# A row softmax with tiles in three buffers: later first store and 16 KB packets for the last stores

## The chip, the cores and the metric

The kernel runs on one core of a Trainium2 chip. The metric is the device time of one execution in microseconds (us), and the median of several is quoted. A profile is one traced execution, so its span differs from the median by a few microseconds.

## The reference

```
batch, seq, vocab = 16, 256, 32768          # 4096 rows of float32
scaled = logits / temperature               # temperature = 1.0
scaled = scaled - scaled.max(axis=-1, keepdims=True)
exp_scaled = np.exp(scaled)
return exp_scaled / exp_scaled.sum(axis=-1, keepdims=True)
```

536.87 MB are read and as much is written.

## The kernel before

Each row of 32768 is cut into two halves on two neighbouring partitions, so that 64 tiles of 128 partitions x 16384 values (8.39 MB) pass through three buffers. A tile is loaded through SyncE's queue, goes through DVE (VectorE, the maximum) and ACT (ScalarE, the exponential) piece by piece, has its sums joined, is scaled on both engines and is stored through ScalarE's queue. A load into a buffer waits for the store that empties it. Tiles 0 and 63 are loaded in four pieces, and tile 63 is also stored in four; all others move in one transfer of 64 KB per partition.

```
def load(t):
    n = _END if t in (0, G - 1) else _LOAD        # 4096 or 16384 columns
    for s in range(0, W, n):
        nc.sync.dma_start(out=buf[t % _BUFS][:, s : s + n], in_=x[...])

def store(t, a, b):
    nc.scalar.dma_start(out=o[t * P : (t + 1) * P, a:b], in_=buf[t % _BUFS][:, a:b])

def normalise(t):
    for k in range(K):
        nc.vector.tensor_reduce(out=nm[:, k : k + 1], in_=xc, axis=X, op=A.max, negate=True)
        nc.scalar.activation(out=xc, in_=xc, func=Exp, bias=nm[:, k : k + 1], ...)
    # ... the sums of the two halves are joined, f is the factor of each piece ...
    for k in range(K):
        # DVE scales columns a:b, ACT scales b:c
        if t == G - 1:
            store(t, a, c)
    if t < G - 1:
        store(t, 0, W)

for t in range(_BUFS):
    load(t)
for t in range(G):
    normalise(t)
    if t + _BUFS < G:
        load(t + _BUFS)
```

## Time and profile before

| | before |
|---|---|
| median of 3 runs | 2516.56 us |
| span of the profile | 2510.7 us |
| DVE, ACT busy | 63%, 54% |
| queues of loads and stores, share of 16 DMA engines | 49.7%, 49.6% |

Two rows of the page suffice to see what kind of kernel this is: the compute engines are idle for a third to a half of the time and the DMA engines are never idle but at the end. What can be gained has to be sought in the stretches of time in which the DMA engines move less than their steady rate.

### The profile page before, as it was taken

The numbers are of one execution on the slowest core, as the hardware profiler recorded it, in microseconds if no ns is written. First come the engines' busy times: TensorE is split into PE (matmuls) and PEld (weight loads), VectorE is DVE, ScalarE is ACT, GpSimd is POOL, SyncE is SP. The second block draws the span as 40 slices with busy tenths as digits, with TensorE's granted clock in tenths as the row PEclk, the third lists the DMA queues.
The fourth block names the chain that finished last, engine by engine and source line by source line (L and its number), as shares of the span: only waits on it lengthen the run. The fifth ranks groups of instructions, "written<-read, shape, count | busy, mean of one in ns | idle before, by whom it ended". The sixth has DMA issues, their size and how long they took to land.

```text
span 2510.7 us, 2617 instructions
## 1 busy us (share of the span) xinstructions
DVE 1575.7 (63%) x1216; ACT 1368.1 (54%) x895; POOL 0.2 (0%) x4
## 2 busy tenths in 40 slices
DVE  6465766657656666576665665766656657666573
ACT  6445646546455465564554645645546456465463
POOL 0000000000000000000000000000000000000000
DMA  9999999999999999999999999999999999999996
GB/s 401 389 427 434 433 433 434 434 433 434 435 433 434 434 432 423 434 434 432 434 434 433 434 433 433 434 434 434 433 434 434 434 433 434 432 427 434 434 427 296
DMA packets 19748, 1073.91 MB, mean 428 GB/s; under 512 B 2192, under 2 KB 2192, under 8 KB 2192
## 3 DMA queue, kind: packets, MB, share of 16 engines
q1 hardware_dynamic: 10080, 536.88, 49.7%
q10 hardware_dynamic: 9648, 536.88, 49.6%
q14 instruction: 20, 0.16, 0.0%
HBM read 536.87 MB, written 536.87 MB: 428 GB/s over the span
## 4 chain that ended last, share of the span: by engine, by line
DMA 72%; DVE 17%; ACT 9%; another core or an unknown queue 2%; issue 0%; SPq 0%; ACTq 0%
DMA x<-in_logits_dram 36%; DMA out_dram<-x 35%; DVE nm L99 12%; ACT x L106 7%; DVE x L135 4%; ACT x L139 2%; DVE f L131 0%; ACT ee L116 0%; DVE rS L130 0%; DVE Sh L78 0%; DVE ttj L119 0%; DVE Sh L75 0%; SPq L62 0%; ACTq L68 0%
## 5 line engine op out<-in xcount | busy, mean ns | idle before, releaser
L99 DVE TENSOR_REDUCE nm<-x 128x1 f32<-128x4096 f32 x318 | 1117.6, 3579 | 701.6 <-DMA x<-in_logits_dram 701.6
L106 ACT ACTIVATE x<-x,nm 128x4096 f32<-128x4096 f32 x318 | 965.4, 3036 | 1043.5 <-DVE nm L99 1043.5
L139 ACT ACTIVATE x<-x,f 128x2048 f32<-128x2048 f32 (+1 forms) x194 | 371.2, 1975 | 75.1 <-DVE f L131 73.7
L135 DVE TENSOR_SCALAR x<-x,f 128x4096 f32<-128x4096 f32 (+2 forms) x194 | 372.2, 1975 | 2.5 <-DVE f L131 0.2
L119 DVE CUSTOM_DVE_ANT_0 ttj<-ee,ssum 128x5 f32<-128x5 f32 (+1 forms) x64 | 10.6, 166 | 196.7 <-ACT ee L116 196.7
L106 ACT ACTIVATION_READ_ACCUMULATOR x<-x,nm 128x1 f32 x318 | 59.3, 186 | 0.0
L116 ACT ACTIVATE ee<-nm,nMh 128x5 f32<-128x5 f32 (+1 forms) x64 | 18.2, 284 | 0.0
L131 DVE TENSOR_SCALAR f<-ee,rS 128x5 f32<-128x5 f32 (+1 forms) x64 | 14.8, 231 | 2.2
L130 DVE RECIPROCAL rS<-Sh 128x1 f32<-128x1 f32 x64 | 10.5, 164 | 2.2
L78 DVE TENSOR_TENSOR nMh<-nMh 128x1 f32<-128x1 f32 x64 | 10.2, 159 | 2.2
L78 DVE TENSOR_TENSOR Sh<-Sh 128x1 f32<-128x1 f32 x64 | 10.2, 159 | 2.2
L114 DVE TENSOR_REDUCE nMh<-nm 128x1 f32<-128x5 f32 (+1 forms) x64 | 10.1, 157 | 2.2
L75 DVE STREAM_SHUFFLE Sh<-Sh 128x1 f32<-128x1 f32 x64 | 9.7, 151 | 0.0
L75 DVE STREAM_SHUFFLE nMh<-nMh 128x1 f32<-128x1 f32 x64 | 9.7, 151 | 0.0
L106 ACT ACT_TABLE_LOAD x1 | 1.3, 1283 | 8.1 <-DMA x<-in_logits_dram 8.1
L119 DVE DVE_READ_ACCUMULATOR2_ANT Sh<- 128x1 f32 x64 | 5.2, 82 | 0.0
L75 DVE LOAD_MASK_SELECT nMh<-nMh x64 | 0.9, 14 | 2.8
L75 DVE LOAD_MASK_SELECT Sh<-Sh x64 | 0.9, 14 | 2.8
L170 POOL MEMSET const-bfloat16-1.0<- 128x1 bf16 x1 | 0.1, 102 | 0.0
L170 POOL MEMSET const-uint8-127<- 128x1 uint8 x1 | 0.1, 102 | 0.0
L170 POOL MEMSET const-float32-0.0<- 128x1 f32 x1 | 0.1, 99 | 0.2 <-issue 0.2
L170 POOL MEMSET const-float32-1.0<- 128x1 f32 x1 | 0.1, 99 | 0.0
## 6 DMA issues: line engine op xcount, KB each, us to landing
x<-in_logits_dram SPq DMA_DIRECT2D x8, 2048.0 KB, 23.7
out_dram<-x ACTq DMA_DIRECT2D x4, 2048.0 KB, 10.7
out_dram<-x ACTq DMA_DIRECT2D x63, 44.3
x<-in_logits_dram SPq DMA_DIRECT2D x62, 43.6
```

The costliest lines, as they stand in the source:

```text
L75: nc.vector.stream_shuffle(out=v[:, j + 1 : j + 2], in_=v[:, j : j + 1], mask=mask)
L78: nc.vector.tensor_tensor(out=v[:, j + 1 : j + 2], in0=v[:, j : j + 1], in1=v[:, j + 1 : j + 2], op=op,)
L99: nc.vector.tensor_reduce(out=nm[:, k : k + 1], in_=xc, axis=X, op=A.max, negate=True)
L106: nc.scalar.activation(out=xc, in_=xc, func=Exp, bias=nm[:, k : k + 1], scale=inv_t, accum_out=ssum[:, k : k + 1],)
L114: nc.vector.tensor_reduce(out=nMh[:, 0:1], in_=nm, axis=X, op=A.min)
L116: nc.scalar.activation(out=ee, in_=nm, func=Exp, bias=nMh[:, n_rounds : n_rounds + 1], scale=-1.0)
L119: nc.vector.tensor_tensor_reduce(out=ttj, in0=ee, in1=ssum, scale=1.0, scalar=0.0, op0=A.mult, op1=A.add, accum_out=Sh[:, 0:1],)
L130: nc.vector.reciprocal(out=rS, in_=Sh[:, n_rounds : n_rounds + 1])
L131: nc.vector.tensor_scalar_mul(out=f, in0=ee, scalar1=rS)
L135: nc.vector.tensor_scalar_mul(out=xs[:, a:b], in0=xs[:, a:b], scalar1=f[:, k : k + 1])
L139: nc.scalar.activation(out=xs[:, b:c], in_=xs[:, b:c], func=Copy, scale=f[:, k : k + 1])
L170: nc = _bacc.Bacc("TRN2", target_bir_lowering=False, num_devices=1)
```

## The change

The intent is to keep the first store out of the way of the first loads, and to let the last load and the last stores share the DMA engines evenly. Store 0 is put behind the first exponential of tile 1 in ScalarE's program. The stores of tiles 61 and 62 go in four transfers of 16 KB per partition. The loads are called one step later, which changes nothing in SyncE's order.

```
+_FINE_STORES = 3
     def store(t: int, a: int, b: int) -> None:
-        nc.scalar.dma_start(
-            out=o[t * P : (t + 1) * P, a:b], in_=buf[t % _BUFS][:, a:b]
-        )
+        n = _END if t >= G - _FINE_STORES else b - a
+        for s in range(a, b, n):
+            nc.scalar.dma_start(
+                out=o[t * P : (t + 1) * P, s : s + n],
+                in_=buf[t % _BUFS][:, s : s + n],
+            )
 ...   (in the loop of exponentials)
+            if t == 1 and k == 0:
+
+                store(0, 0, W)
 ...
-        if t < G - 1:
+        if 0 < t < G - 1:
             store(t, 0, W)
 ...
-            if t + _BUFS < G:
-                load(t + _BUFS)
+            if t and t + _BUFS - 1 < G:
+                load(t + _BUFS - 1)
```

## The prediction

> **What bounds the kernel now.** I read the page first, because it says in two lines that this is a transfer problem: DVE is busy 63% and ACT 54% of the span, while the DMA row is at 9 in all but the last of 40 slices, and the two queues together fill 99.3% of what 16 DMA engines could do.
>
> ```profile
> DVE 1575.7 (63%) x1216; ACT 1368.1 (54%) x895; POOL 0.2 (0%) x4
> ...
> GB/s 401 389 427 434 433 433 434 434 433 434 435 433 434 434 432 423 434 434 432 434 434 433 434 433 433 434 434 434 433 434 434 434 433 434 432 427 434 434 427 296
> ...
> q1 hardware_dynamic: 10080, 536.88, 49.7%
> q10 hardware_dynamic: 9648, 536.88, 49.6%
> ```
>
> The GB/s row shows where anything is to be had. The plateau is 434; the second slice (389) and the last (296) stand out, and the first holds the launch. All bytes, 1073.76 MB, at 434 GB/s take 2474 us, against a span of 2510.7: only 36.6 us are not plateau, and no compute saving can matter. So I cut the span into stretches (columns: window, length, busy time of each engine with instruction counts, clock, DMA share, GB/s).
>
> ```profile
> 40.00:104.00 64.00, 37.33 (x22) 28.95 (x18) 0.00 (x0) 1.00 0.95 365
> 104.00:160.00 56.00, 31.88 (x34) 30.43 (x22) 0.00 (x0) 1.00 1.01 437
> 160.00:2418.00 2258.00, 1432.26 (x1105) 1243.01 (x815) 0.00 (x0) 1.00 1.00 433
> 2418.00:2448.00 30.00, 24.67 (x20) 21.35 (x14) 0.00 (x0) 1.00 0.97 416
> 2448.00:2474.00 26.00, 12.92 (x3) 11.40 (x6) 0.00 (x0) 1.00 0.90 386
> 2474.00:2490.00 16.00, 8.62 (x14) 6.40 (x5) 0.00 (x0) 1.00 0.05 22
> ```
>
> Two holes. Between 40 and 104 us the rate is 365 although DMA is 95% busy: (434-365)/434 x 64 = 10.2 us lost to slow packets, not to idleness. Between 2474 and 2490 DMA is idle: (434-22)/434 x 16 = 15.2 us. The timeline of the end names the second hole:
>
> ```profile
> 2447.85 13.06 DVE L99 TENSOR_REDUCE nm<-x 128x1 f32<-128x4096 f32 x3
> 2448.01 0.34 ACTq L68 DMA_DIRECT2D out_dram<-x  x1
> ...
> 2477.43 4.42 DVE L99 TENSOR_REDUCE nm<-x 128x1 f32<-128x4096 f32 x1 [16.51 <-DMA x<-in_logits_dram]
> ...
> 2488.78 0.34 ACTq L68 DMA_DIRECT2D out_dram<-x  x1
> ```
>
> Three of the last tile's four pieces are reduced by 2460.9, then DVE waits 16.5 us for the fourth, and the first store of the last tile is issued 11.35 us after that piece (2488.78 - 2477.43). By then the store of tile 62 (issued 2448.01) is through, so nothing fills the DMA engines. Why is piece four late? The DMA view of 2420 to 2432, while the last load and the store of tile 61 share the engines (columns: packets, MB, share):
>
> ```profile
> q10 hardware_dynamic: 64, 4.19, 80.8%
> q1 hardware_dynamic: 64, 1.05, 20.4%
> ```
>
> Equal numbers of packets, but a store packet is 64 KB and a load packet of the last tile 16 KB: the load gets a fifth of the bytes. The same recurs after 2450 against the store of tile 62. In the DMA records 13 of 16 engines finish piece four within 5.5 us of the first, the last three 14.9, 17.8 and 25.7 us after it. They had lagged by 5 to 7 us in the preceding tiles and met the 64 KB stores again.
>
> **What the Trainium skill says.** "DMA: Bandwidth & Descriptors", section "Queues, rings and completion order": each DMA engine goes round-robin between the queue rows it has work for and switches only at packet boundaries. The trace agrees: 64 packets against 64 above. Section "Where 436 GB/s comes from" gives 435.2 GB/s as the ceiling of the port fabric; the plateau of 433 to 437 is it, so the middle cannot improve. Section "Rules for kernel authors" says that spreading DMAs over issuing engines buys no bandwidth; here the queues stay SyncE and ScalarE before and after, so I give that nothing. No page I found explains 365 GB/s at 95% busy.
>
> **The change part by part.** The order listing shows SyncE's sequence of loads unchanged: moving the call for the next load after the tile that follows keeps the same buffers and the same wait on the same store. DVE does not change. On ACT, one store moves and two become four pieces each. Bytes are equal.
>
> Part one, fine stores of tiles 61 and 62 (63 already had four): six more issues at 0.34 us, 2.0 us on an ACT queue that waits anyway; 16 KB packets move 425 to 431 GB/s in the trace where they run alone, against 434, which over some 25 MB is well under 1 us. The gain: the last load is issued around 2415.2 to 2418.0 and its data start near 2418. Now packets are equal, so it gets half of 434. On the three late engines the previous load ends at 2420; from there their shares of the last load and of store 61 are 2 x 0.524 MB at 27.1 GB/s an engine (434/16), 38.7 us, so piece four lands near 2458 instead of 2477. Adding 11.35 us, the first store of tile 63 is issued near 2470, with 1.5 us to its first packet 2471.5. The thirteen prompt engines then have their share of store 62 done near 2450.5 + 19.3 = 2470, a gap of 1.5 us; the late three get it done near 2458 + 19.4 = 2477.5 and have no gap. The last 8.39 MB take 19.4 us (0.524 MB an engine): 2497, and the landing 2497.5. Against 2510.7 that is **-13 us**. It is below the 15.2 us of the hole because the late engines end it.
>
> Part two, the held store. Store 0 is issued at 38.28 and its packets appear as load 2 begins; from there to 104 both directions are slow: in the trace's records the packets take 2.9 us (load) and 2.7 us (store) in place of 2.418. After the change it comes behind the first exponential of tile 1, which starts at 46.49 and lasts 3.71, so it is issued near 50.3, 12 us later. Load 2 (42 to 61 alone at 434) keeps the engines full meanwhile, so holding costs no idle time: 10 us x 434 = 4.3 of its 8.39 MB pass alone. The mixed stretch shrinks from some 44 us to some 20, and the two streams no longer start together. If the slowness belongs to that lock-step start, 10.2 us come back, and the lag of three engines with it (up to 6 us at the end, since the slowest engine ends the kernel). If slowness belongs to the first so many microseconds of mixed traffic, load 3 with store 1 will pay it later and nothing is won. I choose 6 of a possible 16 us. Sum: 13 + 6 = 19, from 2516.6 to **2497 us**, -0.8%.
>
> **Rivals.** First: only the tail gains; the slow stretch moves from 42-104 to about 52-120. For it speaks a second slow patch in the records at about 94 to 102, when load 3 meets store 1 at another phase; against it, that in 2258 us of mixed traffic afterwards the rate is 433. It makes 2503. Second: both come back in full, the engines stay in step, and the tail is one solid stream: 2516.6 - 13 - 16 = 2488. Third: equal shares help the load but delay store 61 and store 62, and the hole shifts instead of closing. The DMA work is conserved, and store 62 still has 2458 to 2477 to fill on the late engines, so I expect at most 2 us of gap; were half the hole left, some 7 us less gain, 2504. Fourth: the held store delays load 3 and thereby starves tile 3. Load 3 waits for store 0, which would land near 81 instead of 91.5, when its load is issued now, as there is less to share with; the buffer cycle (store 44.2, load 43.5, compute 28, sum 116 = three tiles of 38.6) has slack only in DMA queueing, and DMA is never empty, so I see no loss; if wrong, up to +10, 2507.
>
> **Range and chances.** The tail is arithmetic on measured packets, good to some 4 us; the start is nearly a coin toss between 0 and 16. That gives 2486 to 2506. A gain of 2% would need 50 us where only 36.6 are off the plateau, launch and first landing included, so faster by 2% is all but excluded; slower by 2% needs a new stall of 50 us that I cannot see.
>
> **What would show it.** Right: the windows after show no 22 GB/s stretch between the last load and the last store; DVE's wait for the last piece falls from 16.5 us to 10 or less; in the stretch where load 63 meets store 61, packets and bytes of both queues are equal; the stores of 61 and 62 are eight issues more of 2048 KB; the rate at 40 to 104 rises above 400. Wrong: the hole stays with equal shares (piece four was late for another reason); the second slice of the GB/s row stays below 400 or the third falls (slow mixed traffic only moved); or a plateau slice falls below 430.

## The result

| | before | after |
|---|---|---|
| median of 4 runs each | 2516.01 us | 2497.87 us |
| lowest to highest | 2514.04 to 2518.52 | 2495.30 to 2502.61 |
| span of the profile | 2510.7 us | 2493.4 us |

The ratio is 0.993, with a 95% interval of 0.9912 to 0.9947. The kernel is 18 us faster and within 2% of before, as predicted.

First the page of the changed kernel, the row of GB/s in 40 slices and the two queues:

```profile
GB/s 421 433 424 436 435 437 424 436 434 437 424 436 435 437 424 436 433 428 435 434 430 433 434 436 427 433 436 431 429 435 437 423 435 437 427 431 437 425 429 379
...
q10 hardware_dynamic: 10512, 536.88, 49.9%
q1 hardware_dynamic: 10080, 536.88, 49.9%
```

The second slice rose from 389 to 433 and the last from 296 to 379. But the middle, which was at 432 to 435 in all but a few slices, now has slices of 423 to 429 again and again. The stretches of time of the changed kernel (same columns as in the prediction; the windows at the end are moved to where its last tile is):

```profile
40.00:104.00 64.00, 49.24 (x38) 42.70 (x28) 0.00 (x0) 1.00 1.00 426
104.00:160.00 56.00, 24.62 (x19) 21.35 (x14) 0.00 (x0) 1.00 1.00 430
160.00:2410.00 2250.00, 1427.73 (x1102) 1238.33 (x812) 0.00 (x0) 1.00 1.00 433
2413.00:2443.00 30.00, 26.63 (x20) 21.35 (x14) 0.00 (x0) 1.00 1.00 429
2443.00:2464.00 21.00, 15.75 (x8) 10.44 (x5) 0.00 (x0) 1.00 1.01 432
2464.00:2474.00 10.00, 4.99 (x10) 7.88 (x8) 0.00 (x0) 1.00 0.41 174
```

The slow stretch at 40 to 104 is gone: 426 in place of 365, worth (426-365)/434 x 64 = 9.0 us. The hole at the end is smaller, not closed: 10 us at 174 cost (434-174)/434 x 10 = 6.0 us, where the prediction said 1.5 on most engines and nothing on the late ones. The DMA view of the changed kernel, 2420 to 2432, answers to the 64 against 64 packets of before (packets, MB, share; a record of 4 bytes per engine and transfer is counted too):

```profile
q1 hardware_dynamic: 184, 2.75, 53.5%
q10 hardware_dynamic: 176, 2.42, 47.3%
```

Packets are about equal and so, now, are bytes: 2.75 MB of the last load against 2.42 MB of the store. Before it was 1.05 against 4.19. The last engine's share of piece four is in 1.1 us after the first engine's, in place of 25.7. So the even sharing worked, and yet a hole is left. ScalarE's timeline at the end of the changed kernel (start, duration, instruction, idle time before it) says why:

```profile
2437.55 0.34 ACTq L71 DMA_DIRECT2D out_dram<-x  x1
2439.03 1.99 ACT L146 ACTIVATE x<-x,f 128x2048 f32<-128x2048 f32 x1
2439.82 13.70 ACTq L71 DMA_DIRECT2D out_dram<-x  x3
2453.56 3.71 ACT L110 ACTIVATE x<-x,nm 128x4096 f32<-128x4096 f32 x1 [12.54 <-DMA x<-in_logits_dram]
...
2471.52 0.34 ACTq L71 DMA_DIRECT2D out_dram<-x  x1
```

Each issue takes 0.34 us, but the last three of tile 62 span 13.70 us, and behind them ScalarE begins the last tile's first exponential only at 2453.56, when the last piece of the load has landed. What it waits for stands in the listing of the compiled program. A transfer raises a completion semaphore, a counter, when it has landed. The program hands out eight of them in turn, named DMAHW0 to 7; the last load's pieces raise 7, 0, 1 and 2, and the four stores of tile 62, which come eight transfers later, get the same and wait for them:

```
445 L71 DMACopy out_dram<-x_60 128x4096 [waits DMAHW7_49,DVE_49]
446 L71 DMACopy out_dram<-x_60 128x4096 [waits DMAHW0_49,DVE_49]
447 L71 DMACopy out_dram<-x_60 128x4096 [waits DMAHW1_49,DVE_49,Activation_49]
448 L71 DMACopy out_dram<-x_60 128x4096 [waits DMAHW2_49,Activation_49]
```

The trace agrees to a tenth of a microsecond. The second line is the last piece of the load in the view of the chain that ended last (issue and time to landing); it lands at 2411.84 + 41.26 = 2453.10, and the fourth store is issued 0.08 us later. The third is issued at 2443.46, and piece three had landed at 2443.36.

```profile
2443.46 0.34 ACTq L71 DMA_DIRECT2D out_dram<-x  x1
...
2411.84 41.26 DMA x<-in_logits_dram
...
2453.18 0.34 ACTq L71 DMA_DIRECT2D out_dram<-x  x1
```

In the kernel before, 67 stores in place of 73 were spread so that no store met such a wait late. The same wait held tile 61's third store too, from 2403.4 until tile 62's load had landed (2412.99; issue at 2413.08). There it delayed no exponential: the first maximum of tile 62 was ready only at 2417.4. The four exponentials of the last tile, which could have followed the load piece by piece, now run one after another from 2453.56 to 2468.34, and the first store of that tile is issued at 2471.52: 18.4 us after the last piece landed (2453.1), against 11.35 before.

### The profile page after: what moved, and what is told of

Same layout as the page of the kernel before. It is cut to its first block, busy times and chain, and to the rows that moved or that the text cites. A ratio compares the mean times of both kernels' runs of the same rounds, so it can differ in the third digit from the quotient of the medians.

```text
span 2493.4 us, 2622 instructions
## 1 busy us (share of the span) xinstructions
DVE 1575.8 (63%) x1216; ACT 1367.7 (55%) x895; POOL 0.2 (0%) x4
## 4 chain that ended last, share of the span: by engine, by line
DMA 75%; DVE 15%; ACT 9%; issue 0%; SPq 0%; DVEq 0%; ACTq 0%
DMA x<-in_logits_dram 38%; DMA out_dram<-x 37%; DVE nm L103 11%; ACT x L110 7%; DVE x L142 3%; ACT x L146 2%; DVE f L138 0%; SPq L63 0%; ACT ee L123 0%; DVE rS L137 0%; DVE Sh L82 0%; DVE ttj L126 0%; DVE Sh L79 0%; DVEq L191 0%; ACTq L71 0%
## 5 line engine op out<-in xcount | busy, mean ns | idle before, releaser
L126 DVE CUSTOM_DVE_ANT_0 ttj<-ee,ssum 128x5 f32<-128x5 f32 (+1 forms) x64 | 10.6, 166 | 203.0 <-ACT ee L123 203.0
L123 ACT ACTIVATE ee<-nm,nMh 128x5 f32<-128x5 f32 (+1 forms) x64 | 18.1, 283 | 0.0
L137 DVE RECIPROCAL rS<-Sh 128x1 f32<-128x1 f32 x64 | 10.5, 164 | 2.2
L82 DVE TENSOR_TENSOR nMh<-nMh 128x1 f32<-128x1 f32 x64 | 10.2, 160 | 2.2
L82 DVE TENSOR_TENSOR Sh<-Sh 128x1 f32<-128x1 f32 x64 | 10.2, 159 | 2.2
## 6 DMA issues: line engine op xcount, KB each, us to landing
x<-in_logits_dram SPq DMA_DIRECT2D x8, 2048.0 KB, 18.4
out_dram<-x ACTq DMA_DIRECT2D x61, 44.3
```

Of the source, the lines that this page charges most:

```text
L82: nc.vector.tensor_tensor(out=v[:, j + 1 : j + 2], in0=v[:, j : j + 1], in1=v[:, j + 1 : j + 2], op=op,)
L123: nc.scalar.activation(out=ee, in_=nm, func=Exp, bias=nMh[:, n_rounds : n_rounds + 1], scale=-1.0)
L126: nc.vector.tensor_tensor_reduce(out=ttj, in0=ee, in1=ssum, scale=1.0, scalar=0.0, op0=A.mult, op1=A.add, accum_out=Sh[:, 0:1],)
L137: nc.vector.reciprocal(out=rS, in_=Sh[:, n_rounds : n_rounds + 1])
```

## The experiments

Two yardsticks made the runs comparable although the time up to tile 62 varies by some 15 us between the profiles. The **tail** is the span less the start of DVE's first reduction of tile 62, which is the moment its load has landed; the **front** is that start itself. The slow packets of the middle are counted from the trace's DMA records: what 64 KB packets between 160 and 2400 us took above the usual 2.418 us each, summed and divided by 16 engines.

| profile | store 0 | stores 61, 62 | front | tail | slow packets in the middle |
|---|---|---|---|---|---|
| before | at once | 64, 64 KB | 2420.0 | 90.7 | 5.1 |
| e6 | at once | 64, 64 KB | 2422.0 | 90.7 | 6.0 |
| e10 | at once | 64, 64 KB | 2422.4 | 90.5 | 8.2 |
| e2 | at once | 16, 16 KB | 2426.3 | 80.5 | 13.5 |
| e11 | at once | 16, 16 KB | 2421.2 | 80.6 | 9.0 |
| after | held | 16, 16 KB | 2413.0 | 80.4 | 8.3 |
| e8 | held | 16, 16 KB | 2416.6 | 80.0 | 11.1 |
| e5 | held less | 16, 16 KB | 2417.5 | 80.2 | 13.1 |
| e7 | held more | 16, 16 KB | 2416.9 | 80.1 | 11.6 |
| e1 | held | 64, 64 KB | 2419.9 | 90.3 | 13.4 |
| e9 | held | 16, 64 KB | 2411.2 | 83.6 | 6.3 |
| e4 | held | 16, 32 KB | 2416.2 | 78.8 | 11.4 |
| e3 | held | 16, 16 KB by SyncE | 2418.5 | 79.1 | 13.6 |

More can be read from the front. Front less slow packets is 2414.2 to 2416.0 in the three profiles with store 0 at once and coarse stores, 2412.2 and 2412.8 at once with fine stores, 2406.5 for e1, and 2404.4 to 2405.5 in the seven with store 0 held and tile 61's store fine. So the slow packets account for nearly all of the scatter of the fronts, and without them the hold is worth some 8 us. Nor is the front free of the fine stores: before the front, DVE waits for tile 62's load 10.5 to 10.6 us in the four profiles with coarse stores and 8.6 to 9.2 in the nine in which tile 61's store is fine, and the 16 engines' shares of that load land within 7.0 to 7.6 us in the former, 3.8 to 4.7 in the latter. These 1.7 us of the fine stores' gain the tail doesn't see. One line each of before and after:

```profile
2419.97 17.46 DVE L99 TENSOR_REDUCE nm<-x 128x1 f32<-128x4096 f32 x5 [10.51 <-DMA x<-in_logits_dram]
2413.01 17.46 DVE L103 TENSOR_REDUCE nm<-x 128x1 f32<-128x4096 f32 x5 [8.74 <-DMA x<-in_logits_dram]
```

### The two parts alone

e1 takes the fine stores back:

```
-_FINE_STORES = 3
+_FINE_STORES = 1
```

> The changed kernel with the fine stores of tiles 61 and 62 taken back: only the first store is held. Theory (the parts add up; the start gave about 7 us, as the last landing of the load of tile 62 came 7.1 us earlier): 2516 - 7 = about 2509 us; 40 to 104 us at 420 GB/s or more; the hole before the last tile's stores and the DVE wait of 16 us for the last piece stay. Rival (the hold is worth its full 10 us, the middle gives nothing back): 2506. Rival (all gain was the tail): 2516.

Measured: 2509.96 us against 2515.34 of before in the same call, ratio 0.9979 (0.9966 to 0.9991). The theory's 2509 fits. The start is repaired (426 GB/s) and the end is as in the kernel before, with DVE waiting for the last piece:

```profile
2477.00 4.42 DVE L103 TENSOR_REDUCE nm<-x 128x1 f32<-128x4096 f32 x1 [16.18 <-DMA x<-in_logits_dram]
```

e2 takes the hold back:

```
-            if t == 1 and k == 0:
-                store(0, 0, W)
-        if 0 < t < G - 1:
+        if t < G - 1:
```

> The changed kernel with the first store not held: only the fine stores. Theory (17 us of the profiled difference minus 7 for the start): about 2506 us; 40 to 104 us at 365 GB/s again; ACT held some 13 us in the issue of tile 62's stores. Rival (fine stores alone give my predicted 13): 2503. Rival (fine stores pay only together with engines in step, which the hold gives): 2512 or more.

Measured: 2503.43 us against 2515.34, ratio 0.9959 (0.9947 to 0.9972), 373 GB/s at 40 to 104, and ScalarE held 13.77 us in the issue of tile 62's stores. The fine stores alone give some 10 to 12 us. The median is that of the first rival (2503) rather than the theory's 2506; the interval, 7 to 13 us, holds both. The second rival, 2512 or more, is out. The tails of the table say it more sharply: 90.3 to 90.7 in four profiles with coarse stores, 80.0 to 80.6 in six with fine ones, so 10 us whatever the start did, and with the 1.7 us of the front some 12.

### What holds ScalarE at the end

e3 issues tile 62's stores from SyncE, which has nothing else to do by then:

```
-            nc.scalar.dma_start(
+            (nc.sync if t == G - 2 else nc.scalar).dma_start(
```

> The changed kernel with tile 62's four stores issued by SyncE instead of ScalarE. The program hands out eight completion semaphores in turn, and each transfer waits for the one eight before it: the third and fourth store of tile 62 wait for the third and fourth piece of the last load, and ScalarE stands in that wait and cannot start the last tile's exponentials. Theory: with the wait moved to SyncE, the exponentials start behind their reductions, the last tile's first store is issued some 11.35 us after the last piece lands in place of 18.5, the 6 us hole closes: about 2491 us, against 2498 of the changed kernel. Rival (the exponentials are late for another reason, or the engines that lag end the kernel anyway): 2497 to 2499.

Measured: 2499.74 us, ratio 0.9943 (0.9929 to 0.9956): no gain in time; the theory's 2491 fell. Yet the steps before went nearly as the theory had it. The wait moved to SyncE, where the four issues span 14.02 us. The stretch that answers to the hole follows, and the last tile's reductions (DVE is busy without a break and never waits for the last piece):

```profile
2443.01 14.02 SPq L71 DMA_DIRECT2D out_dram<-x  x4
...
2460.00:2470.00 10.00, 6.05 (x13) 8.33 (x6) 0.00 (x0) 1.00 0.99 424
...
2446.36 17.39 DVE L103 TENSOR_REDUCE nm<-x 128x1 f32<-128x4096 f32 x4
```

From the landing of tile 62's load to the first store of tile 63 it is now 2470.66 - 2418.47 = 52.2 us, against 2471.52 - 2413.01 = 58.5 in the changed kernel. From the landing of the last piece (2456.63) it is 14.0 us and not the theory's 11.35, because DVE is still at its reductions until 2463.75. But the tail shrank only from 80.4 to 79.1. The hole of 6.0 us was on the average engine; with it closed, the engines that lag end the kernel. The records show it: in the changed kernel the last store lands on all 16 engines within 0.2 us, because all of them had stood idle for it; in e3 fourteen engines end within 0.5 us and the last 4.7 us after the first. Of 6 us some 5 go to that lag, which is the second half of the rival. One thing stays untested: e3 also puts tile 62's stores behind the last load in SyncE's queue, and what that does to the lag is not separated here.

e4 leaves the stores on ScalarE and halves their number:

```
-        n = _END if t >= G - _FINE_STORES else b - a
+        n = min(b - a, {G - 3: _END, G - 2: 2 * _END, G - 1: _END}.get(t, b - a))
```

> The changed kernel with tile 62's store in two pieces of 32 KB packets in place of four of 16 KB, still from ScalarE. By the compiled program the two wait for the first and second piece of the last load, which land before the stores are ready. Theory (the wait for semaphores): ScalarE isn't held, first store of the last tile some 11.35 us after the last piece; the load gets a third in place of half against these packets, so piece four lands 1 to 3 us later: 2492 to 2495. Rival (the hold on ScalarE is the hardware queue being full, not the semaphore): the hold stays at about 13 us and the time at 2498.

Measured: 2496.84 us, ratio 0.9928 (0.9916 to 0.9941), tail 78.8; the time lies between the theory's range and the rival. The two issues together take 1.66 us, so ScalarE isn't held. Half as many issues could also fill a queue less; what settles it is that in the changed kernel the third and fourth issue come 0.1 us after the landings that their semaphores name. The wait was for the semaphores, not for a full queue. The load pays for the larger packets with a wait, as expected:

```profile
2443.02 1.66 ACTq L71 DMA_DIRECT2D out_dram<-x  x2
...
2460.70 4.42 DVE L103 TENSOR_REDUCE nm<-x 128x1 f32<-128x4096 f32 x1 [3.54 <-DMA x<-in_logits_dram]
```

The tail is 1.6 us shorter than the changed kernel's; in the timed runs this cannot be told from it.

e9 makes only tile 61's store fine:

```
-        n = _END if t >= G - _FINE_STORES else b - a
+        n = _END if t == G - _FINE_STORES else b - a
```

> The changed kernel with only tile 61's store in 16 KB packets; tile 62's is one transfer of 64 KB packets again, and tile 63's four pieces are as ever. ScalarE then isn't held by semaphores. Theory (equal packets against both stores are needed, since the engines that lag still have pieces of the last load to take when store 62 starts): the last piece lands later than in the changed kernel by 5 to 15 us on the last engines, DVE waits for it again, time 2500 to 2506. Rival (only the meeting with store 61 matters): 2495 to 2498.

Measured: 2499.18 us, ratio 0.9939 (0.9923 to 0.9956), at the edge below the theory's range and above the rival's. The tail, 83.6, decides for the theory: 3.2 us longer than with both stores fine, 7 us shorter than with none. The last engine's share of piece four is 9.2 us behind the first's, and DVE waits again:

```profile
2461.32 4.42 DVE L103 TENSOR_REDUCE nm<-x 128x1 f32<-128x4096 f32 x1 [9.16 <-DMA x<-in_logits_dram]
```

Hence about 7 of the tail's 10 us are from tile 61's store and 3 from tile 62's, and those 3 are with ScalarE's hold subtracted. The front's 1.7 us are tile 61's as well, since DVE's wait for tile 62's load is 8.70 us in e9.

### What makes the start slow

e5 holds store 0 by six small copies in place of the exponential:

```
+        if t == 0:
+            for _ in range(6):
+                nc.scalar.activation(out=scratch, in_=xs[:, 0:512], func=Copy, scale=1.0)
         if t < G - 1:
             store(t, 0, W)
```

(Left out of the cut: the tile `scratch`, and the change's hold of store 0, which is taken back.)

> The changed kernel, but the first store held by six small ScalarE copies (about 4 us) in place of 8.2 us, so its first packets should fall after the second 64 KB packet of load 2 on each engine, in place of the first (before) or the third (after). Theory (the slow stretch comes only of both streams starting together on engines in step): 40 to 104 us at 420 GB/s or more, time 2498 to 2501. Rival (what matters is how far the load is ahead of the store in its rows, and two packets is as bad as one): 380 or less, and about 2503 like the fine stores alone. In between (400): the offset acts gradually.

Measured: median 2498.97 us, ratio 0.9956 (0.9921 to 0.9991; one of four runs took 2521.72 and widens it). In the profile the store is issued 3.1 us later than in the kernel before (38.28), and that is enough for the full rate:

```profile
41.41 0.38 ACTq L73 DMA_DIRECT2D out_dram<-x  x1
...
40.00:104.00 64.00, 46.32 (x37) 41.70 (x31) 0.00 (x0) 1.00 0.99 426
```

e6 is the kernel before with two tiles exchanged, so that store 0 meets a load from other addresses at the same moment:

```
+    at_tile = list(range(G))
+    at_tile[2], at_tile[34] = 34, 2
-                in_=x[t * P : (t + 1) * P, s : s + n],
+                in_=x[at_tile[t] * P : (at_tile[t] + 1) * P, s : s + n],
```

with the same index in the store.

> The kernel before, with tiles 2 and 34 exchanged in the order of work: the load that meets store 0 then reads 256 MiB further up (32 tiles of 8 MiB), at unchanged timing. Theory (timing and step, not a particular pair of addresses): 40 to 104 us stays at 365 to 375 GB/s and the time within 3 us of before, 2515. Rival (the pair of tile 0 and tile 2 collides in HBM): 420 or more in that window, 2506 to 2510.

Measured: 2514.26 us against 2514.37, ratio 1.0 (0.9986 to 1.0014). The window stays slow, so it isn't that pair of tiles:

```profile
40.00:104.00 64.00, 37.30 (x22) 28.95 (x18) 0.00 (x0) 1.00 0.97 369
```

e7 holds until the third exponential (`k == 2` in place of `k == 0`).

> The changed kernel with the first store held until the third exponential of tile 1 (issue near 55.2 us in place of 46.5), so after five to six of load 2's eight packets. Theory (any start that is not together with load 2's is as good, and DMA stays fed until load 2 ends at 61): 420 or more at 40 to 104, 2496 to 2500 as the changed kernel. Rival (the offset decides packet by packet): the window falls below 400. Rival (too late: an idle gap before the store's first packet): a gap of 1 us or more near 61.

Measured: 2498.76 us, ratio 0.9941 (0.9924 to 0.9958), issue at 55.33 us, 426 GB/s. With issues at 41.4, 46.5 and 55.3 us all at 425 or 426 and those at 38.3 at 365 to 376 in five profiles (e10 and e11 among them), the slow stretch depends on store 0 meeting load 2 at its very start, which in all these kernels is near 42 us: in the records of before, the first store packets begin at 44.3 us, after one packet of load 2 on each engine, and in e5 at 46.5, after two. No experiment shows the mechanism behind that.

### What varies in the middle

e8 is the changed kernel again.

> The changed kernel unaltered, on the chip of this call, to have its spread beside the variants: 2495 to 2502, ratio 0.993. Its profile should show again a start of 420 or more, and by the theory that the loss in the middle is a matter of chance from run to run, a loss of full rate between 160 and 2400 us anywhere from 5 to 15 us (it was 9.7 in the first profile of it).

Measured: 2497.85 us, ratio 0.9928 (0.9915 to 0.9942), as before. e10 and e11 were looks at the kernel before and at e2:

> The kernel before, unaltered, for a second profile of it. By slow 64 KB packets between 160 and 2400 us (time above 2418 ns each, summed over 16 engines and divided by 16) the first profile lost 5.1 us there, the profiles with the held store 8.3 to 13.6. If the middle's loss comes of engines being kept in step by the hold: 4 to 7 us again. If it is chance from run to run: anything up to 14.

> The kernel with fine stores and no hold once more: its first profile lost 13.5 us in the middle by the same sum although its start is that of the kernel before. In-step theory: that profile was an exception, now 4 to 7 us. Chance: anything from 5 to 14.

Slow packets in the middle came to 8.2 us in e10 and 9.0 in e11, both above the 4 to 7 of the in-step theory. Over all profiles the five with store 0 at once have 5.1 to 13.5, mean 8.4; the eight with a hold 6.3 to 13.6, mean 11.1. The means are 2.7 us apart and the ranges cover each other, so that the hold costs something in the middle is likely at most, not shown.

No version beats the changed kernel by more than the spread: e4, the best, has the same ratio.

## Why the prediction was right, and where not

The total was right: -19 predicted, -18.1 measured, and the rates and the even packets went as said. Each part came near its number, but steps inside both failed, and errors of opposite sign helped: that is partly luck.

**The fine stores.** Predicted -13, all of it after tile 62's load; measured there -10.2 (tail 90.6 to 80.4), and -1.7 more because that load itself landed earlier, which the prediction did not see ("the previous load ends at 2420" was kept from before). That makes some -12, as between e1 (ratio 0.9979) and the changed kernel (0.993). The even sharing did what the working said: piece four was to land 38 us after tile 62's load and landed 2453.1 - 2413.0 = 40.1 after it. The step that failed is the cost line "six more issues at 0.34 us, 2.0 us on an ACT queue that waits anyway", and with it "Adding 11.35 us": the issues cost a wait of 13 us inside an instruction stream that had exponentials behind it, and the first store came 18.4 us after the last piece. In the tail this cost little, 1.3 us by e3 and 1.6 by e4. The listing of the waits could have shown it before the run; I read the order of the instructions and not what each waits for. The other half of the step held: once the wait is removed (e3), the late engines end the kernel, and the tail of 79.1 is close to the 77.5 that the prediction's figures make (2497.5 - 2420). The rest of the difference stays open.

**The held store.** Predicted -6, "nearly a coin toss" between 0 and 16. Locally 9.0 us came back at 40 to 104, of the 10.2 named. Fronts less slow packets put it at 8.5 us with coarse stores (e1 against the three) and 7.6 with fine ones. The slow packets of the middle took more in the profiles with a hold, 2.7 us on average, which can be chance. In timed runs e1 gives 5 us over before, and e8 some 8 over e2; they agree within their intervals. The prediction's 6 was a choice between 0 and 16 and had no such sum behind it, so its agreement is partly luck. Two steps in it failed. The issue was to come "behind the first exponential", near 50.3; it came at 46.52, together with the start of that exponential, so it did not wait for the exponential ahead of it to end (nor in e7, 55.33 beside 55.32):

```profile
46.52 3.71 ACT L110 ACTIVATE x<-x,nm 128x4096 f32<-128x4096 f32 x1 [8.24 <-DVE nm L103]
46.52 0.38 ACTq L71 DMA_DIRECT2D out_dram<-x  x1
```

By e5 and e7 this was without effect. And "the lag of three engines with it" did not come back: in the changed kernel too, the landing of one load was spread over 7.4 us by tile 10, so the lag does not need the slow start. One reading of records was loose: the stores' 64 KB packets begun between 42 and 104 us took 2.57 us on average, not 2.7, and from 88 to 92 only store packets began, at the full 2.418; loads took 2.94, as said. And that the plateau is the fabric's ceiling of 435.2 GB/s is an inference: the stretch at 437 lies a little above it.

**The signs.** Of those for right, all came but one: the 22 GB/s stretch gave way to one of 174. Of those for wrong, plateau slices fell below 430, down to 423, and the third slice from 427 to 424; before had such slices too (423, 427), only fewer. That the slow start only moved is not what this shows, with 426 GB/s at 40 to 104 us and 430 from there to 160.

**The rivals.** The first (the slow stretch only moves) fell: 430 GB/s at 104 to 160. The second (both in full, engines in step) fell: the engines did not stay in step, and a hole was left. The third (the hole shifts instead of closing) is what happened in the result, with 6.0 us of hole left against its "at most 2", but by the semaphores and not by the order of the stores. The fourth fell: load 3 was issued at 81.64, as the text said, in place of 91.52, and nothing starved.

## What to carry to other kernels

When two queues share the DMA engines packet by packet, give the transfer that the end waits for packets as large as its rival's; here that was worth some 12 us. Before cutting transfers into more pieces, list what each issue waits for: where completion semaphores are handed out in turn, a piece can wait for the transfer eight places before it, and whatever its engine should compute next waits too. And when an idle stretch is an average over engines, look at the slowest engine before counting it as gain: of 6 us closed in e3, the tail of the profile saw about one and the timed runs none.

## What the Trainium skill lacked or had wrong

- "DMA: Bandwidth & Descriptors", section "Issuing engines are not separate DMA queues", says that issuing from several engines only saves the sequencer's issue time. "Perfetto Trace Analysis", section "DMA Instruction — HWDGE (DVE, Sync)", does have the semaphore wait on the issuing sequencer, which is free for its next instruction only after the issue. What neither page has is what this costs an engine that also computes: 13.70 us for three issues of 0.34 us on ScalarE, with the last tile's exponentials behind them; in e3 the four issues took 14.02 us on SyncE instead and ScalarE was not held.
- "DMA: Bandwidth & Descriptors", section "Queues, rings and completion order", has packets of about 9 to 17 descriptors as the unit of the round-robin. In the changed kernel's records of the start the 16 engines move by turns 16 load records and 16 store records of 64 KB each, so one partition's row was the unit here (and in before 64 records of 16 KB against 64 of 64 KB in 12 us at the end).
- No page has the slow start: with store and load beginning together on engines in step, 365 to 376 GB/s at 95 to 99% busy; with the store 3.1 us later, 426.
- No page has the slow packets after a switch: in e1, 14 store packets that began near 1245 us took 3.0 to 3.5 us in place of 2.418, just as a load had landed on 15 of the 16 engines.
- "DMA: Bandwidth & Descriptors", section "Latency and other measured facts", has engines 7 and 15 as usually slower than the others, without a figure, and guesses at a cause in transfers issued by GpSimd. Here all loads and stores are issued by SyncE and ScalarE, and 4 to 8 us lie between the first and the last of 16 engines on one transfer (tile 62's load, all profiles). The records don't name the engine, so whether it is one of those two is open.
